# Two edits to a two-layer decoder trunk: adding transfers ordered behind GpSimd's sums, and one thread for a pair of stick-breaking heads

## The chip, the cores and the metric

The kernel runs on one NeuronCore of one Trainium2 chip. The metric is the device time of one execution in microseconds; of several runs the median is given. A core has five engines with a queue each: TensorE (PE, with its weight loads shown as PEld), VectorE (DVE), ScalarE (ACT), GpSimd (POOL) and SyncE (SP), which here only issues transfers. Each engine works through its queue in order. An instruction that waits holds up all that stands behind it on the same engine.

## The reference

Two layers over x of 512 tokens by 1024 channels, in float32. The parts that the change touches are the two half-step FFNs of a layer and the stick-breaking heads of its mixer (four heads of 64):

```python
def swiglu(x, w_in, w_out):
    a, b = jnp.split(x @ w_in, 2, axis=-1)
    return (jax.nn.silu(a) * b) @ w_out

# stick-breaking, per block of 128 queries
z = jnp.einsum('bhqd,bhsd->bhqs', q_blk, kf)
log_one_minus = jnp.where(causal, jax.nn.log_sigmoid(-z), 0.0)
after = lax.cumsum(log_one_minus, axis=3, reverse=True) - log_one_minus
weight = jnp.where(causal, jnp.exp(jax.nn.log_sigmoid(z) + after), 0.0)
return jnp.einsum('bhqs,bhsd->bhqd', weight, vf)

for l in range(DEPTH):
    x = layer_norm(ALPHA * x + 0.5 * swiglu(x, ffn1_w_in[l], ffn1_w_out[l]), ...)
    x = layer_norm(ALPHA * x + hybrid_mixer(x, ...), ...)     # stick-breaking, window attention, mLSTM
    x = layer_norm(ALPHA * x + cross_attention(x, mem, ...), ...)
    x = layer_norm(ALPHA * x + 0.5 * swiglu(x, ffn2_w_in[l], ffn2_w_out[l]), ...)
```

## The kernel before

**Number format.** A float32 product is made of three faster ones (`mm3`, line 194 is the matmul): each operand is split into a high part H (a cast on ScalarE, `wH<-raw`) and a low part L (the difference, on VectorE, `wL<-raw,wH`), and H·H, H·L and L·H are added in PSUM. Some products, the value products of attention among them, take plain float32 operands. Nearly all vector work is issued through one wrapper, so it shows as line 121 and is told apart by tile names.

**Buffers.** Weights land in `raw` buffers (three, 1 MB each) by transfers from SyncE's queue, in order; a load waits until the casts and differences of the buffer's last tenant are done. `wH` and `wL` have four buffers each. PSUM has eight banks (`ps`).

**FFN.** The activations stand transposed as `xTH` and `xTL`. The first weights' products over the first 256 tokens are made ahead (`early`), their other half at the start of `body` (matmuls of 256 columns). Then follow f=2 and f=3, two parts each: four products of 24 matmuls of 512 columns, `PLAIN` in the code. From the third pair of column tiles on (`q` = 2 to 10) a product of 2 by 2 blocks is made with seven block products instead of eight (Strassen-Winograd), and that needs sums of blocks:
- `combine` makes sums of activations once per FFN: GpSimd adds H and L of `B11` and `B21` and VectorE those of `B12` and `B22` into four tiles `xr`; VectorE then forms the differences t1 to t4 in place, and each is split into `T` (H on ScalarE, L on VectorE).
- S1, a sum of two weight blocks, is made by transfer: SyncE loads the first block into `sw` (line 692), and GpSimd issues two transfers of 256 KB that add the second block to it. `sw` has two buffers.

There are four FFNs: the first at the start of the program, the others near 787, 1152 and 1911 us of the profile.

**Mixer.** Main-thread projections (matmuls of 512 columns) are interleaved with generator threads: `tick`, called between groups of matmuls, runs a step of a thread whose inputs are ready by the kernel's own clock model. `spawn(gen, banks)` declares the PSUM banks of a thread; threads start in order while their banks fit into `tbanks`. The mLSTM thread takes 3, each stick-breaking head (`sb_head`) 3, each of four window-attention blocks (`swa_block`) 2. A head works on key blocks j = 3 to 0 with W = 512 - 128 j query columns: `front` makes scores z and the soft-plus (three activations on ScalarE, then VectorE, a mask on GpSimd, then a split into `spH`, `spL`), `back` adds the sums over later keys (`nones`, `ntri`) and makes the weights (one activation, one mask), and `av` multiplies with the values `vsb`: a plain float32 matmul with all 128 value columns of the head pair, of which the head's own 64 rows are used.

The order on each engine in the end is set by a scheduler behind these calls, within the dependencies; a dependency of the class NoSync sets an order on one engine without a semaphore.

Of the kernel before, what the change touches and what calls it, by code (L numbers as in the profile page):

```python
# [7 lines left out]
F32 = mybir.dt.float32  # L8
# [4 lines left out]
P = 128  # L13
# [129 lines left out]
class Net:  # L143
# [151 lines left out]
    def behind(self, ins, i):  # L295

        if self.hold is not None:
            self.tc.add_manual_dep(ins.ins, self.hold[i].ins.name, mybir.DependencyInfo(
                mybir.DependencyClass.NoSync, mybir.DependencyReason.DATA), reason="order")

    def proj_T(self, out, W, t0, t1, src=None):

# [218 lines left out]
class Ffn:  # L521
# [109 lines left out]
    def combine(self):  # L631

        n = self.net
        V, G = n.nc.vector, n.nc.gpsimd
        r = {}
        for e, x in ((G, "B11"), (V, "B12"), (V, "B22"), (G, "B21")):
            H, L = self.right(x)
            r[x] = self.two("xr").rearrange("p a (k n) -> p (a k) n", k=2)
            e.tensor_add(r[x], H.bitcast(F32), L.bitcast(F32))
        t1, t2, t3, t4 = r["B11"], r["B12"], r["B22"], r["B21"]  # L640
        V.tensor_sub(t1, r["B12"], t1)
        n.split(*self.T[0], t1)
        V.tensor_sub(t2, r["B22"], t2)
        n.split(*self.T[2], t2)
        V.tensor_sub(t3, t3, t1)
        n.split(*self.T[1], t3)
        V.tensor_sub(t4, t4, t3)
        n.split(*self.T[3], t4)

    def body(self, nxt):  # L650
# [37 lines left out]
        for q in range(self.PLAIN, self.Q):  # L688
            a1, b1 = self.load(q, 0)
            a2, b2 = self.load(q, 1)  # L690
            s = self.ip.tile([P, 4, 256], F32, tag="sw", name=n.nm("sw"), bufs=2)
            nc.sync.dma_start(s, self.block(q, 1, 0))
            for k in (0, 2):
                nc.gpsimd.dma_start(s[:, k:k + 2], self.block(q, 1, 1)[:, k:k + 2], accum_op=ALU.add)
            p1, X = self.p1[q % 2], n.bank()
            self.product(X, a1, "B11", True)
            ACT.copy(p1, X)
            W, Y = n.bank(), n.bank()
            self.product(W, s, "T1", True)
# [43 lines left out]
class Mixer:  # L743
# [18 lines left out]
    def body(self, nxt):  # L762
# [46 lines left out]
        self.natural([(512, 256), (2312, 256)], 512, ev2)  # L809


        n.tbanks = 6
        self.q_sb, self.k_sb = [], []
        for p in range(2):
            for dst, c0, sc, parts in ((self.q_sb, 0, 0.125, "HL"), (self.k_sb, 256, 1.0, "HH")):
                W, b = n.w_cols("sb", w_in, c0 + p * P, p), n.bank()
                n.proj_T(b, W, 0, S)
                dst.append(self.stack(b, sc, parts))
            for h in (2 * p, 2 * p + 1):
                n.spawn(self.sb_head(h), 3)  # L820


        W, b = n.w_cols("ksw", w_in, 1280, n=P), n.bank()
# [101 lines left out]
                evac(2 * half + i, bs[i])  # L925


    def sb_head(self, h):
        n, nc = self.net, self.net.nc
        hp = h // 2  # L930
        qT, kHH, kL = self.q_sb[hp][h % 2], self.k_sb[hp][h % 2], self.k_sb[hp][2 + h % 2]
        r = slice(64 * (h % 2), 64 * (h % 2) + 64)
        z, sp = {}, {}

        sH = [n.m2k("spH", dt=F32R) for _ in range(3)]
        sL = [n.m2k("spL", dt=F32R) for _ in range(3)]

        def front(j):
            q0 = j * P
            W = S - q0  # L940
            z[j] = n.bank()
            n.mm(z[j][:, :W], kHH[:, q0:q0 + P], qT[:, q0:], True, False)
            n.mm(z[j][:, :W], kL[:, q0:q0 + P], qT[:, q0:], False, True)
            a = n.m2k("sc", [P, W])
            nc.scalar.activation(a, z[j][:, :W], AF.Abs)
            nc.scalar.activation(a, a, AF.Exp, scale=-1.0)
            nc.scalar.activation(a, a, AF.Ln, bias=1.0)
            nc.vector.scalar_tensor_tensor(a, z[j][:, :W], 0.0, a, ALU.max, ALU.add)
            nc.gpsimd.affine_select(out=a[:, :P], in_=a[:, :P], compare_op=ALU.is_gt, fill=0.0, base=0,
                                    pattern=[[1, P]], channel_multiplier=-1)  # L950
            o = 256 if j == 3 else 0
            H, L = sH[min(j, 2)][:, o:o + W], sL[min(j, 2)][:, o:o + W]
            nc.vector.tensor_copy(H, a)
            nc.vector.tensor_sub(L, a, H.bitcast(F32))
            sp[j] = (H, L)

        def back(j):
            W = S - j * P
            acc = dict(skip_group_check=True)
            for i in range(3, j, -1):  # L960
                off = (i - j) * P
                n.mm(z[j][:, off:W], self.net.nones, sp[i][0], False, False, **acc)
                n.mm(z[j][:, off:W], self.net.nones, sp[i][1], False, False, **acc)
            n.mm(z[j][:, :W], self.net.ntri, sp[j][0], False, False, **acc)
            n.mm(z[j][:, :W], self.net.ntri, sp[j][1], False, True, **acc)
            w = n.m2k("sc", [P, W])
            nc.scalar.activation(w, z[j][:, :W], AF.Exp)
            nc.gpsimd.affine_select(out=w[:, :P], in_=w[:, :P], compare_op=ALU.is_gt, fill=0.0, base=0,
                                    pattern=[[1, P]], channel_multiplier=-1)
            return w  # L970

        o = n.bank()

        def av(j, w):
            n.mm(o[:, j * P:], self.v_sb[j // 2][:, j % 2, hp * P:(hp + 1) * P], w, j == 3, j == 0,
                 skip_group_check=True)

        yield [qT, kHH, kL]
        front(3)
        front(2)  # L980
        yield sp[3]
        w = back(3)
        front(1)
        yield [w] + list(sp[2])
        av(3, w)
        w = back(2)
        front(0)
        yield [w]
        av(2, w)
        yield sp[1]  # L990
        w = back(1)
        yield [w] + list(sp[0])
        av(1, w)
        w = back(0)
        yield [w]
        av(0, w)
        if hp not in self.ySB:
            self.ySB[hp] = [n.m2k("ySB", dt=F32R) for _ in range(2)]
        n.split(*[y[r] for y in self.ySB[hp]], o[r])


    def swa_block(self, nn):
# [437 lines left out]
```

## Time and profile before

| quantity | value |
|---|---|
| median of 3 runs | 2257.73 us (2257.27 to 2258.74) |
| profiled execution | 2261.62 us |
| its span, first to last instruction | 2259.9 us |
| mean granted TensorE clock | 0.99 |
| DVE busy | 1449.6 us, 64% |
| ACT busy | 928.7 us, 41% |
| POOL busy | 287.4 us, 13% |

Rows of the timeline read: start and duration in us, engine, line, operation, output <- inputs, partitions x elements, count, and in brackets the idle time of the engine before the row with what ended it. Rows of the list of waits read: who waited for whom, us in total, times, longest. Groups read: line, engine, operation, tiles, shape, count, then busy us, mean ns of one, idle us before. Matmuls overlap, so a matmul's duration is longer than its distance to the next; the distances are what TensorE's pace is read from.

### The profile page before, as it was taken

What the parts mean: (1) busy time and instruction counts of PE and PEld (TensorE: products, weight loads), DVE (VectorE), ACT (ScalarE), POOL (GpSimd) and SP (SyncE); (2) the same over time, 40 slices, a digit from 0 to 9 for tenths busy, and PEclk for the clock granted to TensorE, in tenths of its full rate; (3) what the DMA queues carried; (4) which work ended last, traced back from release to release, by engine and by line L of the source; (5) the groups of instructions that cost most, each with busy time, mean ns of one, the idle gap of its engine ahead of it and who ended that gap; (6) DMA issues with size and microseconds to landing.
All of it is one profiled execution on the core that took longest, in us unless ns stands there. A gap on an engine that the chain in (4) does not pass through costs nothing.

```text
span 2259.9 us, 33859 instructions
## 1 busy us (share of the span) xinstructions
PE 2199.5 (97%) x13952; PEld 1980.9 (88%) x13952; DVE 1449.6 (64%) x2016; ACT 928.7 (41%) x1405; POOL 287.4 (13%) x336
## 2 busy tenths in 40 slices
PE   9999999999999989999979999999999999899998
PEld 8999888888788879998869998888887988799987
DVE  6677636777675667773457776367776755777734
ACT  4444512467433234461224454134674332344511
POOL 3110001340010211100121100014300102111000
PEclk9999999999999989999989999999999999899999
DMA  8565433223331446643265554232233215456431
GB/s 227 158 166 150 140 103 96 77 86 112 100 112 56 140 112 159 168 150 103 78 170 149 143 147 136 88 114 74 73 112 112 94 56 145 122 145 167 150 103 47
DMA packets 238143, 273.62 MB, mean 121 GB/s; under 512 B 8058, under 2 KB 196762, under 8 KB 237988
## 3 DMA queue, kind: packets, MB, share of 16 engines
q1 hardware_dynamic: 218404, 252.58, 35.1%
q0 software_dynamic: 19584, 18.88, 5.6%
q8 instruction: 109, 1.79, 0.3%
q14 instruction: 46, 0.38, 0.1%
HBM read 267.76 MB, written 3.67 MB: 120 GB/s over the span
## 4 chain that ended last, share of the span: by engine, by line
PE 83%; DVE 8%; issue 4%; POOL 2%; DMA 1%; ACT 1%; SPq 0%; DVEq 0%; POOLq 0%; ACTq 0%
PE ps L194 81%; DVE wL L121 2%; PE ps L199 2%; DVE x_nat L121 1%; DVE xTL L121 1%; DVE st L121 1%; DMA sw<-in_ffn_w_in_dram 1%; POOL mlrs L121 1%; POOL sw L121 1%; DVE xr L121 0%; DVE T L121 0%; POOL xr L121 0%; DVE Cb L121 0%; DMA x_nat<-in_x_dram 0%; DMA raw<-in_ffn_w_in_dram 0%
## 5 line engine op out<-in xcount | busy, mean ns | idle before, releaser
L121 DVE TENSOR_TENSOR wL<-raw,wH 128x1024 fp32r<-128x1024 f32 (+2 forms) x423 | 504.8, 1195 | 488.9 <-ACT wH L121 484.9
L121 ACT CAST wH<-raw 128x1024 fp32r<-128x1024 f32 (+2 forms) x423 | 439.9, 1044 | 767.7 <-PE ps L194 572.7
L194 PE MATMUL ps<-xTH,wL 128*128 128x256 f32 (+1 forms) x1712 | 525.1, 307 | 38.1 <-DVE wL L121 38.1
L194 PE MATMUL ps<-xTH,wH 128*128 128x256 f32 (+1 forms) x1712 | 527.5, 309 | 1.0 <-ACT sc L121 1.0
L194 PE MATMUL ps<-xTL,wH 128*128 128x256 f32 (+1 forms) x1712 | 525.1, 307 | 2.9 <-DVE xTL L121 2.9
L194 PE MATMUL ps<-T,wH 128*128 128x256 f32 x2304 | 418.6, 283 | 0.0
L194 PEld LDWEIGHTS ps<-xTH,wL 128*128 128x128 f32 x1712 | 330.0, 193 | 55.2 <-DVE wL L121 40.8
L194 PEld LDWEIGHTS ps<-T,wH 128*128 128x128 f32 x2304 | 359.4, 192 | 0.5
L194 PEld LDWEIGHTS ps<-xTL,wH 128*128 128x128 f32 x1712 | 330.2, 193 | 17.9 <-DVE xTL L121 5.3
L194 PEld LDWEIGHTS ps<-xTH,wH 128*128 128x128 f32 x1712 | 329.9, 193 | 14.5 <-ACT sc L121 1.2
L194 PE MATMUL ps<-T,wL 128*128 128x256 f32 x1152 | 326.3, 283 | 0.5 <-DVE wL L121 0.5
L194 PE MATMUL ps<-wH,hH 128*128 128x512 f32 x704 | 274.6, 390 | 0.0
L194 PE MATMUL ps<-wH,hL 128*128 128x512 f32 x704 | 274.5, 390 | 0.0
L194 PE MATMUL ps<-wL,hH 128*128 128x512 f32 x704 | 274.1, 389 | 0.0
L194 PEld LDWEIGHTS ps<-T,wL 128*128 128x128 f32 x1152 | 221.2, 192 | 0.9 <-DVE wL L121 0.7
L121 POOL DMA_DIRECT2D sw<-in_ffn_w_in_dram x72 | 87.7, 1219 | 627.0 <-issue 245.9
L121 POOL TENSOR_TENSOR rs<-ve,mhalf 128x1 f32<-128x1 f32 x32 | 29.8, 931 | 1079.0 <-DVE ve L121 1079.0
L194 PEld LDWEIGHTS ps<-wH,hL 128*128 128x128 f32 x704 | 132.1, 188 | 28.4 <-DVE hL L121 1.3
L194 PEld LDWEIGHTS ps<-wL,hH 128*128 128x128 f32 x704 | 132.2, 188 | 27.3
L194 PEld LDWEIGHTS ps<-wH,hH 128*128 128x128 f32 x704 | 132.2, 188 | 27.2
L121 ACT CAST wH<-sw 128x1024 fp32r<-128x1024 f32 x72 | 75.5, 1048 | 130.9 <-DVE sw L121 90.7
L121 DVE TENSOR_TENSOR wL<-sw,wH 128x1024 fp32r<-128x1024 f32 x72 | 87.9, 1221 | 22.6 <-ACT wH L121 22.5
(243 smaller groups left out, 2964.6 us busy)
## 6 DMA issues: line engine op xcount, KB each, us to landing
raw<-in_ffn_w_in_dram SPq DMA_DIRECT2D x147, 512.0 KB, 6.2
raw<-in_ffn_w_out_dram SPq DMA_DIRECT2D x40, 1024.0 KB, 5.0
raw<-in_ffn_w_in_dram SPq DMA_DIRECT2D x28, 1024.0 KB, 7.1
sw<-in_ffn_w_in_dram SPq DMA_DIRECT2D x36, 512.0 KB, 3.5
sw<-in_ffn_w_in_dram POOLq DMA_DIRECT2D x72, 256.0 KB, 4.6
raw<-in_xattn_w_kv_dram SPq DMA_DIRECT2D x16, 1024.0 KB, 5.6
raw<-in_mix_w_in_dram SPq DMA_DIRECT2D x18, 512.0 KB, 4.0
raw<-in_mix_w_in_dram SPq DMA_DIRECT2D x8, 1024.0 KB, 5.2
```

The lines of the kernel that those rows point to most:

```text
L121: return f(*a, **k)
L194: self.nc.tensor.matmul(out, l, r, start=start, stop=stop, **k)
L199: self.nc.tensor.transpose(out, i, ident)
```

## The change

A helper `order` puts one instruction behind another of the same engine. `combine` keeps its last sum, that of `B21` on GpSimd, and the two adding transfers of each S1 are ordered behind it. In the mixer one thread, `sb_pair`, works on the two heads of a pair: each step does both heads, 64 value columns are used for a head, so that both write their own half of one bank, and one split of 128 rows takes the place of two of 64. A pair declares 5 banks, and `tbanks` goes from 6 to 8.

```diff
+    def order(self, ins, before):
+        self.tc.add_manual_dep(ins.ins, before.ins.name, mybir.DependencyInfo(
+            mybir.DependencyClass.NoSync, mybir.DependencyReason.DATA), reason="order")
...
-            e.tensor_add(r[x], H.bitcast(F32), L.bitcast(F32))
+            i = e.tensor_add(r[x], H.bitcast(F32), L.bitcast(F32))
+        self.summed = i
...
-                nc.gpsimd.dma_start(s[:, k:k + 2], self.block(q, 1, 1)[:, k:k + 2], accum_op=ALU.add)
+                i = nc.gpsimd.dma_start(s[:, k:k + 2], self.block(q, 1, 1)[:, k:k + 2], accum_op=ALU.add)
+
+                n.order(i, self.summed)
...
-        n.tbanks = 6
+        n.tbanks = 8
...
-            for h in (2 * p, 2 * p + 1):
-                n.spawn(self.sb_head(h), 3)
+            n.spawn(self.sb_pair(p), 5)
...
-            n.mm(o[:, j * P:], self.v_sb[j // 2][:, j % 2, hp * P:(hp + 1) * P], w, j == 3, j == 0,
-                 skip_group_check=True)
+            for a in range(2):
+                r = slice(64 * a, 64 * a + 64)
+                n.mm(o[r, j * P:], self.v_sb[j // 2][:, j % 2, hp * P + 64 * a:hp * P + 64 * a + 64], w[a, j], j == 3,
+                     j == 0, skip_group_check=True)
...
+        yield qT + kHH + kL
+        for a in range(2):
+            front(a, 3)
+        yield []
+        for a in range(2):
+            front(a, 2)
+        yield sp[0, 3] + sp[1, 3]
+        for a in range(2):
+            back(a, 3)
+        yield [w[0, 3], w[1, 3]] + list(sp[0, 2] + sp[1, 2])
+        for a in range(2):
+            back(a, 2)
+        o = n.bank()
+        av(3)
+        yield []
+        for a in range(2):
+            front(a, 1)
+        yield [w[0, 2], w[1, 2]]
+        av(2)
...
-        if hp not in self.ySB:
-            self.ySB[hp] = [n.m2k("ySB", dt=F32R) for _ in range(2)]
-        n.split(*[y[r] for y in self.ySB[hp]], o[r])
+        self.ySB[hp] = [n.m2k("ySB", dt=F32R) for _ in range(2)]
+        n.split(*self.ySB[hp], o)
```

What this does to the engines' queues is shown at three places. First GpSimd at the start of the second FFN (the other two later FFNs alike), before; `sw_7717` and `sw_7882` are the first two S1 tiles, `xr` the sums:

```order
L121 TENSOR_TENSOR wL_7416<-raw_7413,wH_7415 128x512
L121 DMA sw_7717<-in_ffn_w_in_dram 128x2x256 x2
L121 DMA sw_7882<-in_ffn_w_in_dram 128x2x256 x2
L121 TENSOR_TENSOR xr_7512<-xTH_7114,xTL_7115 128x1024
L121 TENSOR_TENSOR xr_7518<-xTH_7114,xTL_7115 128x1024
```

and with the change:

```order
L121 TENSOR_TENSOR wL_7410<-raw_7407,wH_7409 128x512
L121 TENSOR_TENSOR xr_7506<-xTH_7108,xTL_7109 128x1024
L121 TENSOR_TENSOR xr_7512<-xTH_7108,xTL_7109 128x1024
L121 DMA sw_7711<-in_ffn_w_in_dram 128x2x256 x2
L121 DMA sw_7876<-in_ffn_w_in_dram 128x2x256 x2
```

The two sums have moved ahead of the four transfers. At the first FFN the sums stood ahead already.

Second, at the same place, VectorE before; `wL_7586` and `wL_7617` are the low parts of f=2's two weights:

```order
L121 TENSOR_TENSOR wL_7586<-raw_7583,wH_7585 128x1024
L121 TENSOR_TENSOR xr_7514<-xTH_7114,xTL_7115 128x1024
L121 TENSOR_TENSOR h_7461<-h_7461,ps_7342 128x512
L121 TENSOR_TENSOR xr_7516<-xTH_7114,xTL_7115 128x1024
L121 TENSOR_TENSOR xr_7512<-xr_7514,xr_7512 128x1024
L121 TENSOR_TENSOR wL_7617<-raw_7614,wH_7616 128x1024
```

and with the change, from the product `h` on (the two `xr` sums stand directly ahead of it); `wL_7580` and `wL_7611` are f=2's:

```order
L121 TENSOR_TENSOR h_7455<-h_7455,ps_7336 128x512
L121 TENSOR_TENSOR xr_7506<-xr_7508,xr_7506 128x1024
L121 TENSOR_TENSOR wL_7580<-raw_7577,wH_7579 128x1024
L121 TENSOR_TENSOR xr_7508<-xr_7510,xr_7508 128x1024
L121 TENSOR_TENSOR T_7448<-xr_7506,T_7447 128x1024
L121 TENSOR_TENSOR xr_7510<-xr_7510,xr_7506 128x1024
L121 TENSOR_TENSOR T_7452<-xr_7508,T_7451 128x1024
L121 TENSOR_TENSOR xr_7512<-xr_7512,xr_7510 128x1024
L121 TENSOR_TENSOR T_7450<-xr_7510,T_7449 128x1024
L121 TENSOR_TENSOR h_7455<-h_7455,ps_7414 128x512
L121 TENSOR_TENSOR T_7454<-xr_7512,T_7453 128x1024
L121 TENSOR_TENSOR wL_7611<-raw_7608,wH_7610 128x1024
```

The first `wL` has moved behind the sums and t1, the second behind the whole chain of differences and T low parts. ScalarE there, with the change; `wH_7674` is the high part of f=3's second weight, whose load reuses the buffer of `raw_7577`, and `T_7453` the fourth T:

```order
L121 CAST wH_7643<-raw_7641 128x1024
L121 CAST T_7451<-xr_7508 128x1024
L121 CAST T_7449<-xr_7510 128x1024
L121 CAST wH_7674<-raw_7672 128x1024
L121 CAST T_7453<-xr_7512 128x1024
```

Before, the same cast of f=3 stood ahead of the third and fourth T. Third, TensorE at that FFN with the change, around the first use of `wL_7611`:

```order
L194 MATMUL ps_7614<-xTH_7108,wH_7610 128x512
L194 MATMUL ps_7614<-xTL_7109,wH_7610 128x512
L194 MATMUL ps_7647<-xTH_7108,wH_7643 128x512
L194 MATMUL ps_7647<-xTL_7109,wH_7643 128x512
L194 MATMUL ps_7678<-xTH_7108,wH_7674 128x512
L194 MATMUL ps_7678<-xTL_7109,wH_7674 128x512
L194 MATMUL ps_7614<-xTH_7108,wL_7611 128x512
```

Before, the matmul with f=2's second `wL` came directly behind the first two rows; now four matmuls of f=3's high parts stand between. In the mixer of the first layer TensorE has, with the change, at the first value product of a pair (`sc` are the heads' weights, `vsb` the values):

```order
L194 MATMUL ps_4512<-spH_4426,ntri 128x256
L194 MATMUL ps_4512<-spL_4432,ntri 128x256
L194 MATMUL ps_4669<-sc_4615,vsb_3914 64x128
L194 MATMUL ps_4669<-sc_4620,vsb_3914 64x128
L194 MATMUL ps_4648<-xTH_3311,wH_4644 128x512
```

Before, such a product was one row with 128 output rows, and the two heads of a pair came to it at different times.

More of the change, by code (lines that the diff above doesn't have):

```diff
@@ L297, in behind @@
         if self.hold is not None:
-            self.tc.add_manual_dep(ins.ins, self.hold[i].ins.name, mybir.DependencyInfo(
-                mybir.DependencyClass.NoSync, mybir.DependencyReason.DATA), reason="order")
+            self.order(ins, self.hold[i])
+    def order(self, ins, before):
+        self.tc.add_manual_dep(ins.ins, before.ins.name, mybir.DependencyInfo(
+            mybir.DependencyClass.NoSync, mybir.DependencyReason.DATA), reason="order")
     def proj_T(self, out, W, t0, t1, src=None):
@@ L925, in natural, with sb_pair, front @@
                 evac(2 * half + i, bs[i])
-    def sb_head(self, h):
+    def sb_pair(self, hp):
         n, nc = self.net, self.net.nc
[L930 to L938, printed above, removed]
+        qT = self.q_sb[hp]
+        kHH, kL = self.k_sb[hp][:2], self.k_sb[hp][2:]
+        z, sp, w = {}, {}, {}
+        sH = [[n.m2k("spH", dt=F32R) for _ in range(3)] for _ in range(2)]
+        sL = [[n.m2k("spL", dt=F32R) for _ in range(3)] for _ in range(2)]
+        def front(a, j):
@@ L939, in front @@
             q0 = j * P
             W = S - q0
[L941 to L948, printed above, removed]
@@ L949, in front @@
-            nc.gpsimd.affine_select(out=a[:, :P], in_=a[:, :P], compare_op=ALU.is_gt, fill=0.0, base=0,
+            z[a, j] = n.bank()
+            n.mm(z[a, j][:, :W], kHH[a][:, q0:q0 + P], qT[a][:, q0:], True, False)
+            n.mm(z[a, j][:, :W], kL[a][:, q0:q0 + P], qT[a][:, q0:], False, True)
+            t = n.m2k("sc", [P, W])
+            nc.scalar.activation(t, z[a, j][:, :W], AF.Abs)
+            nc.scalar.activation(t, t, AF.Exp, scale=-1.0)
+            nc.scalar.activation(t, t, AF.Ln, bias=1.0)
@@ L950, in front @@
+            nc.vector.scalar_tensor_tensor(t, z[a, j][:, :W], 0.0, t, ALU.max, ALU.add)
+            nc.gpsimd.affine_select(out=t[:, :P], in_=t[:, :P], compare_op=ALU.is_gt, fill=0.0, base=0,
                                     pattern=[[1, P]], channel_multiplier=-1)
             o = 256 if j == 3 else 0
[L952 to L955, printed above, removed]
@@ L957, in back @@
-        def back(j):
+            H, L = sH[a][min(j, 2)][:, o:o + W], sL[a][min(j, 2)][:, o:o + W]
+            nc.vector.tensor_copy(H, t)
+            nc.vector.tensor_sub(L, t, H.bitcast(F32))
+            sp[a, j] = (H, L)
+        def back(a, j):
             W = S - j * P
@@ L961, in back @@
                 off = (i - j) * P
[L962 to L968, printed above, removed]
-                                    pattern=[[1, P]], channel_multiplier=-1)
@@ L970, in back @@
-            return w
-        o = n.bank()
-        def av(j, w):
-            n.mm(o[:, j * P:], self.v_sb[j // 2][:, j % 2, hp * P:(hp + 1) * P], w, j == 3, j == 0,
-                 skip_group_check=True)
[L978 to L996, printed above, removed]
-        if hp not in self.ySB:
-            self.ySB[hp] = [n.m2k("ySB", dt=F32R) for _ in range(2)]
-        n.split(*[y[r] for y in self.ySB[hp]], o[r])
+                n.mm(z[a, j][:, off:W], n.nones, sp[a, i][0], False, False, **acc)
+                n.mm(z[a, j][:, off:W], n.nones, sp[a, i][1], False, False, **acc)
+            n.mm(z[a, j][:, :W], n.ntri, sp[a, j][0], False, False, **acc)
@@ new lines, in back, with av @@
+            n.mm(z[a, j][:, :W], n.ntri, sp[a, j][1], False, True, **acc)
+            t = n.m2k("sc", [P, W])
+            nc.scalar.activation(t, z[a, j][:, :W], AF.Exp)
+            nc.gpsimd.affine_select(out=t[:, :P], in_=t[:, :P], compare_op=ALU.is_gt, fill=0.0, base=0,
+                                    pattern=[[1, P]], channel_multiplier=-1)
+            w[a, j] = t
+        def av(j):
+            for a in range(2):
+                r = slice(64 * a, 64 * a + 64)
+                n.mm(o[r, j * P:], self.v_sb[j // 2][:, j % 2, hp * P + 64 * a:hp * P + 64 * a + 64], w[a, j], j == 3,
+                     j == 0, skip_group_check=True)
@@ L1002, in swa_block @@
+        yield sp[0, 1] + sp[1, 1]
+        for a in range(2):
+            back(a, 1)
+        yield []
+        for a in range(2):
+            front(a, 0)
+        yield [w[0, 1], w[1, 1]]
+        av(1)
+        yield sp[0, 0] + sp[1, 0]
+        for a in range(2):
+            back(a, 0)
+        yield [w[0, 0], w[1, 0]]
+        av(0)
+        self.ySB[hp] = [n.m2k("ySB", dt=F32R) for _ in range(2)]
+        n.split(*self.ySB[hp], o)
     def swa_block(self, nn):
```

## The prediction, made before the changed kernel was run

> **What bounds the kernel now.** The page comes first: TensorE is busy for nearly the whole span, so the question is where it is not, and where it is busy at a lower clock.
>
> ```profile
> PE 2199.5 (97%) x13952; PEld 1980.9 (88%) x13952; DVE 1449.6 (64%) x2016; ACT 928.7 (41%) x1405; POOL 287.4 (13%) x336
> ```
>
> Next the list of waits over the whole span. Two rows belong together: three waits of VectorE for GpSimd's sums `xr`, and eight waits of TensorE for low parts `wL` of weights, which VectorE makes.
>
> ```profile
> DVE xr L121 <- POOL xr L121: 47.4, 3, 16.4
> PE ps L194 <- DVE wL L121: 38.6, 8, 11.5
> ```
>
> Third, the chain of work that ended last, at the start of the second FFN (start, duration, what).
>
> ```profile
> 779.43 1.30 POOL sw L121
> 780.73 3.41 issue
> ...
> 795.86 2.84 POOL xr L121
> 798.76 3.24 issue
> 802.00 1.21 DVE wL L121
> ```
>
> GpSimd issues four adding transfers into `sw` one after another, and only then sums `xr`; VectorE waits in order for that sum, and the `wL` that TensorE needs stands behind. Fourth, TensorE's timeline at the three later FFN starts. The first 512-column matmul of f=2, the waits, and the first 256-column matmul behind the 96 of f=2 and f=3:
>
> ```profile
> 787.37 0.40 PE L194 MATMUL ps<-xTH,wH 128*128 128x512 f32 x1
> 803.26 0.79 PE L194 MATMUL ps<-xTH,wL 128*128 128x512 f32 x1 [9.81 <-DVE wL L121]
> 812.94 0.50 PE L194 MATMUL ps<-xTH,wL 128*128 128x512 f32 x1 [1.06 <-DVE wL L121]
> 823.50 0.28 PE L194 MATMUL ps<-xTH,wH 128*128 128x256 f32 x1
> ...
> 1152.08 0.40 PE L194 MATMUL ps<-xTH,wH 128*128 128x512 f32 x1
> 1179.32 0.50 PE L194 MATMUL ps<-xTH,wL 128*128 128x512 f32 x1 [1.60 <-DVE wL L121]
> 1189.89 0.28 PE L194 MATMUL ps<-xTH,wH 128*128 128x256 f32 x1
> ...
> 1911.18 0.40 PE L194 MATMUL ps<-xTH,wH 128*128 128x512 f32 x1
> 1938.40 0.50 PE L194 MATMUL ps<-xTH,wL 128*128 128x512 f32 x1 [2.18 <-DVE wL L121]
> 1950.59 0.28 PE L194 MATMUL ps<-xTH,wH 128*128 128x256 f32 x1
> ```
>
> In the order of before, 50 of the 96 stand ahead of the second wait and 46 from it on. Those 46 took 823.50 - 812.94 = 10.56 us, 0.23 each; 50 at that pace are 11.5 us. They took 25.57, 27.24 and 27.22 us. **Lost: 14.1 + 15.7 + 15.7 us**, and at the third start 1.6 more, since its last 46 took 12.19. Together **47.1 us**, more than the 38.6 of waiting, because the clock falls too. Columns here: stretch, its length, busy time of PE, PEld, DVE, ACT, POOL with counts, then granted clock, DMA share, GB/s.
>
> ```profile
> 795.90:809.40 13.50, 6.13 (x14) 4.79 (x15) 10.67 (x8) 5.06 (x6) 5.08 (x3) 0.50 0.36 97
> 1936.20:1938.40 2.20, 0.02 (x2) 0.00 (x1) 2.20 (x3) 1.59 (x3) 0.00 (x0) 1.00 0.00 0
> 1939.40:1942.60 3.20, 3.20 (x9) 2.42 (x9) 3.20 (x5) 0.00 (x0) 0.00 (x0) 0.50 0.99 284
> ```
>
> Half clock follows the 10 us wait, and even the one of 2.2 us.
>
> **Part 1, transfers behind the sums.** Nothing is computed more or less. On GpSimd's queue both sums move ahead of four transfers, at three FFN starts; at the first FFN the order already was so. These rows price the new chain, with its counterpart in the first FFN where both engines sum at once:
>
> ```profile
> 25.94 5.74 POOL L121 TENSOR_TENSOR xr<-xTH,xTL 128x1024 f32<-128x1024 f32 x2
> 26.83 5.94 DVE L121 TENSOR_TENSOR xr<-xTH,xTL 128x1024 f32<-128x1024 f32 x2
> ...
> 768.48 1.70 POOL L121 TENSOR_TENSOR wL<-raw,wH 128x512 fp32r<-128x512 f32 x1 [1.03 <-ACT wH L121]
> 781.21 0.60 ACT L121 ACTIVATE h<-ps 128x512 f32<-128x512 f32 x1
> 781.74 1.05 ACT L121 CAST wH<-raw 128x1024 fp32r<-128x1024 f32 x1
> 781.19 0.37 SPq L251 DMA_DIRECT2D raw<-in_ffn_w_in_dram  x1
> 803.13 1.21 DVE L121 TENSOR_TENSOR xr<-xr,xr 128x1024 f32<-128x1024 f32 x1
> 804.27 1.21 DVE L121 TENSOR_TENSOR T<-xr,T 128x1024 fp32r<-128x1024 f32 x1
> ...
> raw<-in_ffn_w_in_dram SPq DMA_DIRECT2D x28, 1024.0 KB, 7.1
> ...
> DMA to landing us min/median/max: 3.4/4.6/9.0
> ```
>
> (The last row is that of the tile `sw`, transfers of 256 and 512 KB.) At the second FFN GpSimd is free at 768.48 + 1.70 = 770.2, so its sums end near 776 and VectorE's, side by side with them, near 778. The transfers' first issue was 779.43, when the plain load before them had landed, so holding them behind the sums delays none; SyncE's queue keeps its order.
>
> What is late next? VectorE's order now has the product into `h` first, which needs the SiLU that ends at 781.8. From there: `h` 0.6, t1, and the `wL` of f=2's first part, at 1.14 us a step and 1.21 for the last: it ends at 784.8. Before, that `wL` stood ahead of the sums, and the 1 MB reload of its raw buffer (f=3, second part) was issued at 781.19, as it ended. **The reload now goes out 3.6 us later.** ScalarE takes its `wH` cast ahead of the fourth T, VectorE's fourth T low part waits for that, and f=2's second `wL` stands behind it. So that `wL` is ready at 784.8 + 7.1 (landing) + 1.05 (wH) + 1.05 (T) + 1.2 (T low) + 1.2 (wL) = 796.4. Without the reload VectorE's own steps from 781.8, ten of 1.14 and two of 0.6, would end near 794.5. TensorE reaches this `wL` after 30 matmuls instead of 26, since four H matmuls of f=3 were moved ahead: 787.37 + 30 x 0.23 = 794.3. **A new wait of 2.1 us** takes the place of the old.
>
> Behind the wait VectorE makes the other two `wL` at 1.14 us each while TensorE has 22 matmuls, 5 us, before the next, so the second wait has cover. The first raw load of the next stage (a1) finds its buffer free at 796.4, 66 matmuls or 15 us before its product, twice a 1 MB landing. The adding transfers are issued when they were, and their product comes behind that of a1.
>
> Such a wait is where the half clock was seen to begin: 2.18 brought it, 1.06 and 1.60 did not (46 matmuls in 10.56 and 10.57 behind them). It cost 1.6 there; I take half, 0.8. Three starts lose 2.9 each, and part 1 gives **47.1 - 8.7 = 38.4 us**. Bounds: a landing of 3.4 leaves VectorE's own steps as the bound and almost no wait (47); one of 9.0 makes 4.0 us and the half clock, 5.6 each (30).
>
> [...]
>
> **Part 2, one thread per pair.** TensorE has no slack in the mixer to win back: over its ten stretches from 372 to 635 us it idles 3.4 us.
>
> ```profile
> sum 263.00, PE 259.63 PEld 220.69 DVE 185.25 ACT 135.60 POOL 53.97; mean PE 25.96 PEld 22.07 DVE 18.53 ACT 13.56 POOL 5.40
> ...
> 497.86 1.56 PE L194 MATMUL ps<-sc,vsb 128*128 128x512 f32 x4
> 499.06 0.41 PE L194 MATMUL ps<-spH,nones 128*128 128x128 f32 x1
> ...
> 562.90 0.39 PE L194 MATMUL ps<-wH,memT 128*128 128x512 f32 x1
> 563.22 1.08 PE L194 MATMUL ps<-pT,vsw 128*64 128x512 f32 x4
> 564.23 0.55 PE L199 MATMUL ps<-ident,lg 128*128 128x128 f32 x3
> ...
> 567.58 1.94 PE L194 MATMUL ps<-pT,vsw 128*64 128x512 f32 x8
> 569.45 0.39 PE L194 MATMUL ps<-st,st 128*128 128x256 f32 x1
> ...
> L121 ACT ACTIVATE sc<-sc 128x512 f32<-128x512 f32 x8 | 5.1, 631 | 0.3
> ```
>
> The change leaves the matmuls' number and moving columns as they are; only value operands go from 128 to 64 columns. Each matmul of this type shows as two records. With 128 columns a 512 and a 256 took 1.20 us (497.86 to 499.06), 1.56 ns a column; four heads stream 4 x 1280 columns, 8.0 us a mixer. The window attention already uses 64-column operands in two halves of the output: eight records took 1.87 us, four 1.01, so 1024 columns more cost 0.86 us, 0.84 ns a column: two halves run side by side. The rest is fixed: 0.15 in the four, and 0.09 ahead (0.32 from the matmul before instead of 0.23). Eight visits a mixer: 5120 x 0.84 ns + 8 x 0.24 = 6.2 us; with as much again on the way out as ahead, 6.9. I take 6.7, a gain of **1.3 a mixer, 2.6 us in all**. Bounds: none side by side, 8.0 + 1.9, a loss of 1.9 a mixer; no fixed cost, a gain of 3.7.
>
> [...]
>
> Output splits fall from four of 64 rows to two of 128; they lie beside TensorE's work and I cost them at nothing. The waits are the unknown. Two heads of 512 columns now ask ScalarE for six activations of 0.63, 3.8 us, in a row, and other weights' casts (1.05 each) queue behind or between. Between such fronts and their use stand 30 matmuls of 0.23, 6.9 us, besides the value product; VectorE and GpSimd need some 2 to 3 us behind ScalarE. I take no new wait; at the other end 1.4 us at two steps of two pairs in two layers, 11 us.
>
> **Sum.** The profiled execution took 2261.6 us around its span of 2259.9: 2261.6 - 38.4 - 2.6 = 2220.6. The median of the runs is 3.9 lower, 2257.73, which gives **2217 us**.
>
> **Rivals.**
> - *The reload is hidden* (landing of 5 us or less, or its cast slips): no wait stays, part 1 gives 47, about 2208. Against it: 7.1 is the median of 28.
> - *The new wait is long*: landings of 9 and half clock each time give 30, about 2225; with new waits in the mixer 2230. For it: adding transfers share the DMA engines with the reload, as before.
> - *The operands don't run side by side, or the order doesn't hold*: the first gives 2217 + 6.4 = 2223. For the second, GpSimd's printed order must be wrong, which nothing suggests.
> - *Slower*: the pair thread becomes the bound in the mixer. Its two heads move together, the second pair starts only after the first (5 + 5 banks exceed 8), and the window blocks are left to the end. It would decide from 41 us of new waits, 1 us at each of ten steps of four pairs. Against it: the 11 us above, and 3.4 us of TensorE's idle time in a whole mixer now; price 2260 or more.
>
> **How the numbers follow.** Forecast 0.5, hidden reload 0.15, long wait 0.2, no overlap 0.1, slower 0.03, something else near no change 0.02. The range takes part 1 from 47 down to 30 us and part 2 from 6 gained to 6 lost: 2257.7 - 53 and 2257.7 - 24, 2204 to 2234. About 0.2% is what a measurement of this kernel tells from no change; the chances are 0.95, 0.02 and 0.03.
>
> **What would show it.** Right: at the three starts GpSimd's `xr` begins near 770 and before `sw`; no wait of VectorE for GpSimd's `xr`; TensorE waits 1 to 4 us once for f=2's second `wL`, with ScalarE's `wH` of f=3 behind a DMA; the 64-column products start in pairs. Wrong: a wait near 10 us stays, or TensorE's idle time in a mixer grows by over 5 us.

## The result, and the profile after

The changed kernel takes **2220.06 us** (median of 3 runs, 2219.99 to 2222.72) against 2257.73: a ratio of **0.9836, 95% interval 0.9814 to 0.9858**. The forecast was 2217 us, 2204 to 2234. The profiled execution took 2222.7 us, its span 2221.0. A second series gave 2220.09 and a ratio of 0.9833 (0.9818 to 0.9847).

The page's first part, and the waits of TensorE for low parts of weights over the whole span (times, longest):

```profile
PE 2187.5 (98%) x13952; PEld 1969.1 (89%) x13952; DVE 1446.8 (65%) x2012; ACT 926.0 (42%) x1401; POOL 293.9 (13%) x336
...
PE ps L194 <- DVE wL L121: 9.9, 6, 2.5
```

The 38.6 us of this wait became 9.9, and the row of VectorE's waits for GpSimd's `xr` (47.4 us) is gone from the list. The timeline of GpSimd at the start of the second FFN shows the new order: both sums first, then the adding transfers.

```profile
767.76 1.38 POOL L121 TENSOR_TENSOR wL<-raw,wH 128x512 fp32r<-128x512 f32 x1 [1.35 <-ACT wH L121]
769.09 6.31 POOL L121 TENSOR_TENSOR xr<-xTH,xTL 128x1024 f32<-128x1024 f32 x2
778.54 1.30 POOL L121 DMA_DIRECT2D sw<-in_ffn_w_in_dram  x1 [3.14 <-DMA sw<-in_ffn_w_in_dram]
```

TensorE's timeline at the three later starts has one wait each, and behind it 66 matmuls until the first one of 256 columns:

```profile
795.42 0.50 PE L194 MATMUL ps<-xTH,wL 128*128 128x512 f32 x1 [2.10 <-DVE wL L121]
810.52 0.28 PE L194 MATMUL ps<-xTH,wH 128*128 128x256 f32 x1
...
1147.81 0.50 PE L194 MATMUL ps<-xTH,wL 128*128 128x512 f32 x1 [0.54 <-DVE wL L121]
1162.90 0.28 PE L194 MATMUL ps<-xTH,wH 128*128 128x256 f32 x1
...
1894.99 0.50 PE L194 MATMUL ps<-xTH,wL 128*128 128x512 f32 x1 [2.47 <-DVE wL L121]
1911.70 0.28 PE L194 MATMUL ps<-xTH,wH 128*128 128x256 f32 x1
```

The 66 took 15.10, 15.09 and 16.71 us: only behind the third wait did the clock fall (mean granted clock 1.00, 1.00 and 0.92 over the 22 us around each wait), for 1.6 us more. Lost at the starts are now 2.1 + 0.5 + 4.1 = 6.7 us, against 47.1 before.

Where the rest went shows a table of the stages. A stage runs from the first matmul that waits for its new `xTL` to that of the next stage; "first" is the program's start with the first FFN, and 2 and 1 behind an FFN say which of its layer it is (layers 0 and 1).

```
                first  mixer0 xattn0 ffn2_0 ffn1_1 mixer1 xattn1 ffn2_1   span   median
before         369.86  273.14 119.64 364.71 366.39 273.09 119.62 373.43  2259.9  2257.73
after          367.59  274.35 119.65 352.75 352.38 274.42 119.65 360.19  2221.0  2220.06
after_again    368.18  274.36 119.65 354.08 352.47 272.70 119.66 360.21  2221.3  2220.09
part1_only     369.17  273.17 119.65 351.74 356.13 273.21 119.65 360.31  2223.0  2223.84
part2_only     370.47  274.32 119.63 363.75 365.31 274.38 119.63 372.78  2260.3  2260.88
cast_behind_t4 372.62  272.76 119.65 350.88 350.88 274.39 119.67 356.32  2217.2  2218.17
pair_wide      370.72  276.69 119.65 351.24 352.78 278.16 119.63 358.26  2227.1  2228.01
two_blocks     366.64  282.71 119.64 351.14 352.03 282.89 119.65 356.26  2231.0  2232.91
no_reload      367.35  272.71 119.65 358.07 358.23 272.67 119.64 363.74  2232.0  2234.84
kv3            370.87  270.39 119.64 350.88 352.27 270.33 119.64 356.33  2210.3  2210.28
nine_banks     368.64  271.47 119.63 350.90 352.01 271.44 119.64 356.30  2210.0  2211.78
heads_cast     368.60  273.19 119.65 350.82 352.08 273.12 119.65 356.34  2213.4  2215.15
no_reload_f3   366.77  274.33 119.67 350.68 350.64 274.41 119.64 356.43  2212.6  2214.12
best           368.66  270.41 119.64 350.60 355.49 270.44 119.64 356.44  2211.3  2207.55
```

(us; the columns of stages are from one profiled execution each, the median from the timed runs; nine_banks has one.) The three FFNs gave 12.0 + 14.0 + 13.2 = **39.2 us**, where 38.4 was forecast. By the losses at the starts they should have given 47.1 - 6.7 = 40.4. The 1.2 us in between lie in the first FFN of layer 1 (14.0, where 15.7 - 0.5 = 15.2 were due): VectorE's two scalings of `x_nat`, the last of the layer norm, take 2.43 us beside GpSimd there, and 1.41 at the two other starts, and TensorE waits for them.

```profile
1119.96 2.43 DVE L121 SCALAR_TENSOR_TENSOR x_nat<-x_nat,rs,scr 128x512 f32<-128x512 f32 x2
1120.07 1.78 POOL L121 TENSOR_TENSOR wL<-raw,wH 128x512 fp32r<-128x512 f32 x1 [0.28 <-ACT wH L121]
1122.54 0.63 PE L199 MATMUL ps<-ident,x_nat 128*128 128x128 f32 x4 [1.01 <-DVE x_nat L121]
```

This execution and seven others of the table have this wait at this start (0.98 to 1.01 us); cast_behind_t4 and no_reload_f3 have the order of the transfers and no such wait, and neither have before and part2_only, which are without that order. That the order brings it is likely, and not shown.

The mixers, forecast to shrink by 1.3 each, **grew by 1.2 and 1.3**. The first stage is not to be read: over the runs it spreads from 366.6 to 372.6 us, with half clock at the program's start (8.56 us in the changed kernel) and a late weight near 100 us of 0.4 to 2.9.

What happened in the mixer: the busy times of a window of 263 us of it (length, then PE, PEld, DVE, ACT, POOL, granted clock), VectorE's and ScalarE's timeline near its end, and TensorE's wait there:

```profile
372.00:635.00 263.00, 257.31 (x1483) 216.76 (x1482) 180.26 (x385) 133.49 (x281) 53.39 (x92) 0.99 0.32 97
571.80:575.10 3.30, 3.30 (x10) 2.53 (x9) 3.30 (x7) 0.86 (x2) 0.00 (x0) 0.50 0.89 303
...
564.04 2.49 DVE L121 TENSOR_TENSOR lg<-lg,swden 128x512 f32<-128x512 f32 x4
567.20 2.49 DVE L121 TENSOR_TENSOR lg<-lg,swden 128x512 f32<-128x512 f32 x4
569.60 1.22 DVE L121 TENSOR_TENSOR wL<-raw,wH 128x1024 fp32r<-128x1024 f32 x1
...
564.41 2.93 ACT L121 CAST wH<-raw 128x1024 fp32r<-128x1024 f32 x3
...
570.88 0.50 PE L194 MATMUL ps<-wL,memT 128*128 128x512 f32 x1 [2.21 <-DVE wL L121]
```

TensorE's idle time in the window went from 3.4 to 5.7 us. The largest piece is a new wait of 2.21 us for a value weight of the cross-attention, whose `wL` stands on VectorE behind eight multiplies of window blocks, and half clock follows it. In TensorE's order of before, the 48 logit products of window blocks 1 to 3 are spread over 252 matmuls of the memory's projections (52 us); in that of after they come within 36 (12 us), since beside a pair of 5 banks only one block of 2 fits into 8.

### The profile page after: what moved, and what is told of

It reads as the page before. It is cut to its first block, busy times and chain, and to the rows that moved or that the text cites. A ratio compares the mean times of both kernels' runs of the same rounds, so it can differ in the third digit from the quotient of the medians.

```text
span 2221.0 us, 33874 instructions
## 1 busy us (share of the span) xinstructions
PE 2187.5 (98%) x13952; PEld 1969.1 (89%) x13952; DVE 1446.8 (65%) x2012; ACT 926.0 (42%) x1401; POOL 293.9 (13%) x336
## 4 chain that ended last, share of the span: by engine, by line
PE 86%; DVE 7%; issue 2%; DMA 2%; ACT 1%; POOL 1%; SPq 0%; DVEq 0%; ACTq 0%; POOLq 0%
PE ps L194 84%; PE ps L199 2%; DVE wL L121 2%; DVE x_nat L121 1%; DMA raw<-in_ffn_w_in_dram 1%; DVE xTL L121 1%; POOL mlrs L121 1%; DVE st L121 1%; DVE lg L121 1%; ACT wH L121 0%; DVE Cb L121 0%; DMA x_nat<-in_x_dram 0%; DVE hid L121 0%; ACT e L121 0%; DMA biasD<-scr 0%
```

## Experiments

**Each part alone.** One kernel with the old heads and only the order of the transfers, one with the pair thread and without that order:

```diff
-            n.spawn(self.sb_pair(p), 5)              # part1_only, tbanks 6
+            for h in (2 * p, 2 * p + 1):
+                n.spawn(self.sb_head(h), 3)
...
-                n.order(i, self.summed)              # part2_only
```

> The kernel before with the order of S1's adding transfers alone; the stick-breaking heads stay four threads of one head. Theory (the two parts are independent, the order of the transfers brings the gain, the pair thread costs 1.2 to 1.3 us a mixer): the two later second FFNs and the later first FFN are 352.8, 352.4 and 360.2 us long as in the changed kernel, the mixers 273.1 us as before (274.4 in the changed kernel), in all 2217.5 us, 2.5 below the changed kernel. Rival (the mixers grew by something that the transfers bring, since weights of the mixer are on the same queues): the mixers are 274.4 us here too, in all 2220.

> The changed kernel without the order of S1's adding transfers; only the pair thread is left of the change. Theory: the later FFN starts wait on GpSimd's sums as before (FFNs of 364.7, 366.4 and 373.4 us), the mixers are 274.4 us, in all 2257.7 + 2.5 = 2260. Rival (the pair thread is worth what was forecast, 1.3 us a mixer, and what the mixers lost in the changed kernel comes from the other part): mixers of 271.8 us, in all 2255.

Measured: ratios of 0.9845 (0.9831 to 0.9860) and 1.0005 (0.9994 to 1.0016) to the kernel before. The mixers of the first are 273.17 and 273.21 us, as before; those of the second 274.32 and 274.38, as after; the FFNs go with the transfers. So the parts are independent, the whole gain is the first part's, and by the mixers' stages **the pair thread cost 2.5 us** instead of giving 2.6. The medians alone don't show it: the changed kernel's 2220.06 lies below the 2223.84 of the first, whose forecast of 2217.5 was 6 too low. In the profiles 2.9 us of that are the FFNs, where the new wait came longer (1.10, 2.60 and 2.54 us, with half clock behind two: mean granted clock 1.00, 0.97 and 0.97 over the 62 to 66 us around them), and 1.6 the first stage; the rest is not accounted for.

**Which chain makes the new FFN wait.** The rows of the changed kernel, of SyncE's queue, ScalarE and VectorE:

```profile
783.86 0.37 SPq L251 DMA_DIRECT2D raw<-in_ffn_w_in_dram  x1
...
787.24 1.05 ACT L121 CAST T<-xr 128x1024 fp32r<-128x1024 f32 x1 [1.10 <-DVE xr L121]
790.97 1.05 ACT L121 CAST wH<-raw 128x1024 fp32r<-128x1024 f32 x1 [2.68 <-DMA raw<-in_ffn_w_in_dram]
791.92 1.05 ACT L121 CAST T<-xr 128x1024 fp32r<-128x1024 f32 x1
...
790.53 0.68 DVE L121 TENSOR_TENSOR h<-h,ps 128x512 f32<-128x512 f32 x1
793.00 1.23 DVE L121 TENSOR_TENSOR T<-xr,T 128x1024 fp32r<-128x1024 f32 x1 [1.80 <-ACT T L121]
794.15 3.49 DVE L121 TENSOR_TENSOR wL<-raw,wH 128x1024 fp32r<-128x1024 f32 x3
```

The reload lands 7.1 us after its issue, ScalarE stands 2.68 us before its cast, and VectorE 1.80 before T4's low part. To tell that chain from VectorE's own, the cast is ordered behind T4's:

```diff
+                    if (f, part) == (3, 1):
+                        n.order(n.cast, self.t4)     # self.t4: ScalarE's cast of the last split in combine
```

> The changed kernel with ScalarE's cast wH of f=3's second part ordered behind the fourth T cast, in each FFN. Theory (the new waits at the FFN starts, 2.10, 0.54 and 2.47 us, come from this cast, which waits for a reloaded weight and holds up T4, T4's low part and the next wL): T4's cast can start when its operand is there (about 1.5 us earlier than now), VectorE does T4's low part about 1.9 us earlier, and the three waits go to under 0.3 us each, with them the half clock of 3.4 us behind the third (1.7 us): 5.1 + 1.7 = 6.8 us less, 2213 us. Rival (VectorE's own chain of xr, T and h sets the moment of wL, whatever ScalarE does): the waits stay within 0.5 us of what they are, 2219 to 2220 us. Second rival (the cast, now later, makes f=3's wL late in its turn): the same waits stand one part further on.

Measured: 2218.17 us (2214.26 to 2220.56), ratio 0.9819 (0.9803 to 0.9834). The waits went, and nothing took their place:

```profile
792.95 1.05 ACT L121 CAST T<-xr 128x1024 fp32r<-128x1024 f32 x1 [1.22 <-DVE xr L121]
794.31 1.05 ACT L121 CAST wH<-raw 128x1024 fp32r<-128x1024 f32 x1 [0.31 <-DMA raw<-in_ffn_w_in_dram]
...
796.98 0.50 PE L194 MATMUL ps<-xTH,wL 128*128 128x512 f32 x1 [0.22 <-DVE wL L121]
```

The three FFNs take 350.88, 350.88 and 356.32 us, 7.2 less than after. The median fell by 2 us only, partly because this profile's first stage is 5 us longer than that of after; the stages are the better witness here.

A second way to the same cause, without any order: take the reload away. The weights of f and f + 1 are loaded together, and the loader forgets them when the other part's load comes; here the second uses the buffer they are in, once for all f, once for f=3 alone.

```diff
-        return self.net.w_cols((self.tag, part), self.w_in, part * DFF + f * P, f % 2, share=share)
+        if f % 2 == 0:                               # no_reload; for no_reload_f3: if f != 3
+            W = n.w_cols((self.tag, part), self.w_in, part * DFF + f * P, 0, share=share)
+            self.held[part] = n.raws[((self.tag, part), "c", part * DFF + f * P)]
+            return W
+        return n.prep(self.held[part][:, :, P:], [KT, P], share)
```

> The changed kernel, where the second of two neighbouring column blocks takes its weights from the buffer that both were loaded to, so that the reload of f=3's two parts (and of f=1's, at the later FFN starts) is gone; the order of the casts is left as it is. Theory (the FFN starts wait because the reload for f=3's second part comes late, and ScalarE's cast of it holds up T4): with the operand there early, the waits of 0.5 to 2.6 us go under 0.3 us, 5 to 7 us less than the changed kernel on this chip. Rival (it is the number of casts ahead of T4 on ScalarE, not the reload): one cast of 1.05 us stays ahead of T4, and a wait of about 1 us stays at each start, 2 to 4 us less. The first FFN, where a weight comes late near 100 us (0.4 to 2.9 us over the runs), may gain from fewer transfers as well, by up to 2 us, in either case.

> The changed kernel with the reload taken away for f=3 alone (both parts), so that the later FFN starts up to f=2 stay as in the changed kernel; ScalarE's casts of f=3 stand ahead of T3 and T4 as there or one place earlier still. Theory (the reload's landing holds up the cast, and with it T4 and the next wL): no FFN start waits over 0.3 us for wL, FFNs of 350.9, 350.9 to 352 and 356.3 us, 4 to 7 us below the changed kernel, 2214 to 2216. Rival (the number of casts ahead of T4 matters, not the landing): waits of about 1 us, FFNs of 352 us, 2217 to 2219. The waits for x_nat of the kernel without any reload (2.57 and 2.19 us) do not come, if they came from the start and not from f=3.

Without any reload: 2234.84 us, ratio 0.9895 (0.9881 to 0.9910), 15 us slower than the changed kernel beside it, which neither theory nor rival had. The waits for `wL` at the starts were gone, but 2.57 and 2.19 us for `x_nat`, with 6.8 us of half clock, had come just ahead of them. GpSimd, VectorE and TensorE there, and then VectorE's same row in the changed kernel:

```profile
765.94 5.24 POOL L121 TENSOR_TENSOR xr<-xTH,xTL 128x1024 f32<-128x1024 f32 x2
...
766.15 5.58 DVE L121 SCALAR_TENSOR_TENSOR x_nat<-x_nat,rs,scr 128x512 f32<-128x512 f32 x2
...
769.04 0.66 PE L199 MATMUL ps<-ident,x_nat 128*128 128x128 f32 x4 [2.57 <-DVE x_nat L121]
771.88 0.87 PE L199 MATMUL ps<-ident,x_nat 128*128 128x128 f32 x3 [2.19 <-DVE x_nat L121]
```

```profile
766.58 1.41 DVE L121 SCALAR_TENSOR_TENSOR x_nat<-x_nat,rs,scr 128x512 f32<-128x512 f32 x2
```

With f=1's weights there early, GpSimd reaches its sums 6.2 us into the stage (which begins at 759.71) instead of 7.5, and VectorE, which has one `wL` of 1.65 us more ahead of them, its last two scalings of the layer norm at 6.4 instead of 5.0: they meet, and the scalings take 5.58 us instead of 1.41. With the reload gone for f=3 alone the start stays as it was: 2214.12 us, ratio 0.9798 (0.9781 to 0.9814), no wait for `wL` over 0.3 us at a start, FFNs of 350.68, 350.64 and 356.43. In this kernel the casts of f=3 still stand ahead of T4, some earlier than after, so **the landing made the wait, not the number of casts**.

**The mixer: what the 64 columns are worth.** The same pair thread with all 128 value columns and one bank for each head:

```diff
-                r = slice(64 * a, 64 * a + 64)
-                n.mm(o[r, j * P:], self.v_sb[j // 2][:, j % 2, hp * P + 64 * a:hp * P + 64 * a + 64], w[a, j], j == 3,
+                n.mm(o[a][:, j * P:], self.v_sb[j // 2][:, j % 2, hp * P:(hp + 1) * P], w[a, j], j == 3,
```

> The changed kernel, but the pair's value products take the 128 columns of both heads, one bank for each head, and the rows of the own head are read from each (half the result is left unread, as in the kernel before). Theory (64-column products of the two heads run side by side, which is worth 1.3 us a mixer, and other waits outweighed it): the mixers grow from 274.4 to 275.7 us, in all 2222.7. Rival (side by side is worth nothing, the products' entry and exit cost as much as they save): the mixers stay within 0.3 us of 274.4, in all 2220. The two additional low parts and casts of each pair are 64 rows high and short; both theories put them off TensorE's path.

Measured: 2228.01 us, ratio 0.9865 (0.9851 to 0.9880). The mixers grew by more than either theory had it, to 276.7 and 278.2. Without its idle time and half clock, TensorE's time in a mixer is 269.4 us before, 266.6 after, and 269.8 with 128 columns: the narrow operands are worth **3.2 us a mixer**, not 1.3. In the timeline of the changed kernel the 512-column products of both heads take 1.01 us together:

```profile
506.54 1.08 PE L194 MATMUL ps<-sc,vsb 128*64 128x512 f32 x4
507.55 0.33 PE L194 MATMUL ps<-st,st 128*128 128x128 f32 x1
```

**The mixer: what the wait rests on.** If three blocks at once are too many for VectorE, two at once should mend it. And if only the place of `wL` matters, an earlier preparation should, with three blocks left as they are. Both on the kernel with the cast behind T4, and so is the third, where nine banks are counted, so that a block more runs beside the second pair.

```diff
-            n.spawn(self.swa_block(nn), 2)           # two_blocks
+            n.spawn(self.swa_block(nn), 3)
...
-        n.tbanks = 8                                 # nine_banks, ahead of Xattn.memory
+        n.tbanks = 9
...
-                H, L = n.w_rows("kv", w_kv, k0, 2, D + c * 512, KT)      # kv3
+                while todo and len(got) < 4:
+                    got.append(n.w_rows("kv", w_kv, *todo.pop(0), KT))
+                H, L = got.pop(0)
```

> The kernel with ScalarE's cast behind T4, and each window block counts three banks instead of two, so that two of them run at once instead of three. Theory (the mixers' wait of 2.21 us for a value weight's low part, with the half clock behind it, comes from three window blocks whose logits, 0.40 us a piece, and multiplies, 0.60 us a piece, stand on VectorE ahead of that wL, and from their exponentials ahead of its cast on ScalarE): the wait goes, the mixers fall from 274.4 with half clock (272.8 without) to 270.5 us, the program by 4 to 8 us against the kernel with the cast alone, to 2211. Rival (VectorE and ScalarE have the same work to do before the mixer ends, and the wait only moves): a wait of 1 to 3 us at the out projection, for the fourth block's results, mixers of 272 to 275 us, in all 2217 to 2219.

> The kernel with ScalarE's cast behind T4, and the value weights of the cross-attention prepared three pieces ahead, so that their low parts stand on VectorE behind the first group of four multiplies of a window block instead of the second, and one cast stands ahead of the third block's exponentials on ScalarE. The three window blocks still run at once. Theory (the mixers' wait of 2.21 us is a matter of what stands ahead of wL, two groups of multiplies of 2.4 us each): wL comes about 2.5 us earlier, the wait and the half clock behind it go, mixers of 270.5 us (272.7 now, 274.4 with half clock), the program 4.4 to 7 us below the kernel with the cast alone, 2212. Rival (as with two blocks at a time, the window blocks' results then come late): a wait of 1 to 3 us at the transposes of the multiplied logits or in the out projection, mixers of 272 to 275 us, 2216 to 2218.

> The kernel with ScalarE's cast behind T4, and nine banks counted in the stage of the second pair, so that two window blocks instead of one run beside the pair thread and one block's work is moved ahead, as in the kernel before. Theory (the window blocks came in a heap because five banks of the pair left room for one of them): the wait of 2.21 us falls under 1 us, the mixers to 271 us. Rival (eight banks are all there are, and the pair's products wait for one): waits of 1 us and more between 530 and 550 us, mixers of 274 us and more.

Two blocks at once: 2232.91 us, ratio 0.9888 (0.9872 to 0.9905). The wait of 2.21 us is gone, and the mixers are 8 to 10 us longer. The rival was right and named too small a price: the fourth block's logits come some 45 us later on VectorE, and the out projection stands for its multiplies:

```profile
615.05 2.49 DVE L121 TENSOR_TENSOR lg<-lg,swden 128x512 f32<-128x512 f32 x4
...
615.88 2.50 PE L199 MATMUL ps<-ident,lg 128*128 128x128 f32 x10 [5.64 <-DVE lg L121]
```

Weights three pieces ahead: **2210.28 us** (2209.38 to 2212.05), ratio 0.9787 (0.9774 to 0.9800). VectorE's timeline has `wL` between the two groups of multiplies, TensorE doesn't wait there, and the mixers take 270.39 and 270.33 us. The window is the same 263 us of the mixer as above:

```profile
567.31 2.49 DVE L121 TENSOR_TENSOR lg<-lg,swden 128x512 f32<-128x512 f32 x4
569.72 1.22 DVE L121 TENSOR_TENSOR wL<-raw,wH 128x1024 fp32r<-128x1024 f32 x1
...
572.54 2.49 DVE L121 TENSOR_TENSOR lg<-lg,swden 128x512 f32<-128x512 f32 x4
...
375.30:638.30 263.00, 259.55 (x1500) 218.78 (x1499) 183.93 (x392) 134.39 (x282) 55.22 (x94) 1.00 0.32 97
```

So the wait was a matter of what stands ahead of one instruction, not of how much work there is. Nine banks gave 271.4 us a mixer, with a wait of 0.62 us at the logits instead; the stagger mends it as well, a little less.

**Is the pair thread worth its place?** The old heads with both the order of the transfers and the cast behind T4:

> The kernel before with the order of S1's transfers and ScalarE's cast behind T4, and the four threads of one head: the changed kernel's first part with its new wait mended, without its second. Theory (each mixer loses 2.7 us of TensorE time by the pair thread and gains 2.3 us of waits and, mostly, 1.7 us of half clock): mixers of 273.1 to 273.2 us, FFN starts without a wait over 0.3 us, FFNs of 350.9, 350.9 and 356.3 us, the program within 3 us of the kernel with pair thread and cast, 2216 to 2219; and 3 to 6 us above the kernel with the value weights ahead. Rival (the cast's order rests on the changed kernel's moments and a wait comes back here): an FFN start waits 1 us or more.

Measured: 2215.15 us, ratio 0.9809 (0.9796 to 0.9823). Mixers of 273.19 and 273.12, FFN starts without a wait. In the same series kv3 is 4.9 us faster: with its wait mended the pair thread gives **2.8 us a mixer**. The old heads with the value weights ahead were not run; they have no wait of 0.45 us or more for a `wL` in the mixer that this could take away.

**Repeated, and both mendings together.**

> The changed kernel once more, as a measure for the two others on this chip. In four runs on another chip the same FFN wait was 0.54 to 2.60 us from start to start, and the half clock behind the mixers' 2.21 us came in five mixers of six. Expected: 2220 to 2223 us; FFN waits of 0.5 to 2.6 us, mixers with 2.21 us each.

> The two mendings together on the changed kernel: f=3 takes its weights from the buffer that they are in, and the value weights of the cross-attention are prepared three pieces ahead. Theory (the two new waits are independent of each other): FFNs as in the kernel without f=3's reload (350.7, 350.6 and 356.4 us), mixers as in the one with the weights ahead (270.4 us), 2214.1 - 2 x 3.95 = 2206 us. Rival (the first FFN's start, 366.6 to 372.6 us long from run to run, sets most of the difference between such kernels): 2208 to 2212.

The changed kernel again: waits of 1.77, 0.58 and 2.50 us at the FFN starts, half clock behind two of them; 2.20 and 2.21 us in the mixers, half clock behind one. The last kernel has the order of the transfers, the pair thread, f=3 without reload and the value weights ahead: **2207.55 us** (2207.54 to 2213.06), ratio **0.9771 (0.9758 to 0.9784)**, faster than before and after. It stands 1.6 us above the theory's 2206 and 0.5 below the rival's 2208, so the time doesn't tell the two apart; the profiled execution, 2213 us, is its slowest, with 2.19 us for `x_nat` and half clock at one FFN start. There VectorE's scalings of `x_nat` took 4.59 us beside GpSimd, as in the kernel without reloads:

```profile
1114.92 4.59 DVE L121 SCALAR_TENSOR_TENSOR x_nat<-x_nat,rs,scr 128x512 f32<-128x512 f32 x2
...
1114.92 1.29 POOL L121 TENSOR_TENSOR wL<-raw,wH 128x512 fp32r<-128x512 f32 x1 [0.17 <-ACT wH L121]
1116.17 5.57 POOL L121 TENSOR_TENSOR xr<-xTH,xTL 128x1024 f32<-128x1024 f32 x2
```

Why that collision comes in some kernels and not in others (the first FFN start of layer 1 was free of it in the kernel with f=3's reload gone) was not tried.

## Why the prediction was right, and where it was not

**Part 1, 38.4 us forecast, 39.2 measured; right by its mechanism, the closeness partly luck.** GpSimd's sums begin at 769.1, forecast near 770; its transfers go out 17.0 us into the stage, 16.8 before; VectorE no longer waits for `xr`. The new wait has the place, the chain and the moment that were forecast: TensorE goes on at 795.4 instead of 796.4, in a stage that begins 1.05 us earlier, after 2.10 us instead of 2.1. Two experiments that each take one link out, the cast's place and the landing, take all three waits away.

**The cost of that wait, 2.9 us a start, is a mean of things that vary.** Over the four kernels that have it as it stands (after, its repeat, part1_only, pair_wide) the wait was 0.54 to 2.60 us, and half clock followed five of the twelve. By the method of the prediction after lost 6.7 us, not 8.7; the 1.2 us of layer 1's first FFN, which are not in its sum, took back more than half of that. The rivals *hidden reload* and *long wait* are the ends of this scatter: with the wait away the FFNs are 46.8 us shorter than before (no_reload_f3: 14.0 + 15.8 + 17.0), next to the 47 that the first of them gave.

**Part 2, 2.6 us gained forecast, 2.5 lost measured: two terms were wrong, with opposite signs.**
- "A gain of 1.3 a mixer": TensorE's time without idle fell by 2.8. From the starts of its records, value products with the sums and projections next to them fell by 2.4, the logits by 0.5, and the rest cancels. The old products, put at 8.0, cost more: their tail shows in the sum that follows them (a 128-column product on `spH` held TensorE for 0.22 us in the mean before, 0.25 directly behind a value product, and for 0.07 with the pair thread). By the distances they hold it for 6.6 us of their own and some 2.4 in the records behind them, about 9. The narrow ones came near their price of 6.7: 5.6 of their own and 1.4 at entry and exit, about 7. The rival without overlap fell: with 128 columns the mixers are 2.3 and 3.7 us longer.
- "I take no new wait": this is the step that failed. Idle time grew by 2.3 us a mixer, and half clock cost up to 1.7 more, 4.0 against a gain of 2.8. The prediction looked for waits where the pair thread itself computes, at ScalarE's fronts; outside the window blocks the changes nearly cancel (a wait of 1.29 us for the mLSTM's `hid` came, waits of 0.46, 0.48 and 0.76 for `sc` and `memT` went). The 2.21 us came from what the thread displaced, the window blocks. Its rival *slower* named them ("left to the end") but priced them only as a whole.

**The sum** came within 0.1%: the profiled execution took 2222.7 against 2220.6. Part 2's error of 5.1 us is partly hidden by the first stage (2.3 us shorter, by chance) and part 1 (0.8).

**The clock.** Half clock followed the wait of 2.47 us, and not those of 2.10 and 0.54. Taking half the price for each start came close to the mean, without a reason; how the first two lay on the clock's steps stands in the last section.

## What to carry to other kernels

Where a thread grows, price the threads that it pushes aside: look in the order for work that now comes in a heap, and for a short instruction behind it that TensorE needs. Move that one instruction: to run two blocks at once instead of three made the mixers 8 us longer, to prepare three weights ahead made them 4 shorter. A wait that a repair leaves is worth following once more: here one landing, of data that lay in the next buffer, held two engines.

## What the runs showed of the hardware

**Half clock began on a grid.** In the traces of the kernel before and of the changed kernel all periods of half clock start on one grid of 3.413 us and last one to four of its steps (the last is cut off by the program's end). For the changed kernel, from the trace's clock records:

```
start of half clock, us     8.56   571.76  1670.85  1896.13  2216.98
steps of 3.4133 since first    0   165.00   487.00   553.00   647.00
```

In the kernel before the first starts at 795.82 us, and the others 107, 330, 335 and 428 steps later.

What goes with them is TensorE's idle time within the step of the grid ahead. In these two traces the steps at full clock with 2.18 us idle or more were all followed by half clock (2.18, 2.37, 2.88 and two whole steps before; 2.21, 2.21, 2.27 and one whole step after); none with 1.22 or less was; of the three between, 1.55 (before) and 1.80 (after) were not followed and 1.90 (after, at the program's start) was, and what decides there stays open. The wait of 2.10 us lay across a boundary of the grid, with 1.80 of it in the step from 793.62; of the one of 2.47, 2.27 lay in the step from 1892.72. The mixers' waits of 2.21 us fell each into one step of the changed kernel (from 568.34 and from 1667.44), half clock followed both, and the mixers took 274.35 and 274.42 us. no_reload has two waits of 2.2 us for a `wL` as well and mixers of 272.71 and 272.67, 1.7 less; why half clock stayed away there was not shown.

**VectorE was slower beside GpSimd's sums.** VectorE's two scalings of 128x512 took 5.58 us beside GpSimd's sums (no_reload), 4.59 beside a `wL` and a sum of GpSimd's (best), 2.43 beside a `wL` of 1.78 us and the beginning of a sum (after), and 1.41 at the two other starts of after, where they lay beside GpSimd's rows for less than 0.7 us; its two sums `xr` took 5.94 in the prediction's row beside GpSimd's, where one alone takes 1.22 (median of eight in the kernel before). That GpSimd's work, 1.3 us earlier in the stage in the kernel without reloads, would bring waits of 2.57 and 2.19 us at a start, where the changed kernel waited 2.10, was not expected.
